# A hybrid DeltaNet and retention layer on one Trainium2 core: TensorE's order from the v convolutions to the last merge written out by hand

## The chip, the core and the metric

The kernel runs on one NeuronCore of a Trainium2 chip. Its engines run side by side, each through its own list of instructions in order: TensorE (PE, matrix products; PEld is its weight load), VectorE (DVE), ScalarE (ACT), GpSimd (POOL) and SyncE (SP, which here only issues DMAs). They wait for each other through semaphores. The metric is the device time in microseconds; lower is better.

## What is computed

One layer over 256 context and 1024 latent tokens of width 1024, float32 in and out: a modulated RMSNorm, one input projection, two parallel head groups (gated DeltaNet and retention, each in both directions), an output projection, and a SwiGLU block. The part that matters here is the first head group up to its triangular solves, and the columns of the projection that belong to gates:

```
qkv_a, z, ab, rq, rk, rv, rg = jnp.split(p, splits, axis=-1)
qkv_a = concat([short_conv(qkv_a[:, :CTX_LEN], cw), short_conv(qkv_a[:, CTX_LEN:], cw)])   # 5 taps, then silu
q = l2_normalize(q) * (HEAD_DIM ** -0.5);  k = l2_normalize(k)
...
G = jnp.cumsum(gc, axis=-1)
decay = jnp.where(incl, jnp.exp(G_i - G_j), 0.0)
A = jnp.where(strict, einsum('nbhid,nbhjd->nbhij', kb, kc) * decay, 0.0)
sol = triangular_solve(A + I, rhs)          # per chunk of 64 tokens, head and direction
qk = einsum('nbhid,nbhjd->nbhij', qc, kc) * decay
...
o_gdn = rms_norm(o_f + o_b) * silu(z);   o_ret = head_group_norm(r_f + r_b) * silu(rg)
```

## The kernel before

The 1280 tokens are ten tiles of 128 (0 and 1 the context, 2 to 9 latent). Activations stand as `hhi`/`hlo` and weights as `whi`/`wlo`, two parts of a split float32, so each product is three matmuls. The input projection is made in two forms. **Convolved columns** come from `conv_block` (L605 to L618): twelve blocks of 128 columns (q, k, v of four heads; the v heads are blocks 8 to 11), each in chunks of 256, 512 and 512 tokens; ACT copies the chunk from PSUM into `u` (L608) and, with the middle tap, into `y` (L609), DVE adds the four other taps (L615), ACT applies Silu (L618). **Token-major columns** come from `token_major` (L371 to L373, tile `tm`): ten groups `g` of 256 columns; 2 to 5 are retention's q and k with rotary (`fin_rope`), 6 and 7 the retention gate `rg`, 8 and 9 the gate `z`, both finished with a Silu on ACT (`fin_gate`, L532) into `res`, of which there are two buffers, and stored to DRAM.

`ada_rest` sums a modulation vector: DVE accumulates eight slices of a weight read from DRAM into `acc` (L497, L499), one matmul `gr` (L504) adds across partitions. The last of these, `gr_2313`, and the q transposes `qt` (L686, with squares on ACT, L688) stand just ahead of the section that is changed.

**Preparation** (`pre`, per tile): load `kc` and `qc` (normalised k and q, from DRAM, L659), `kk` = k·kᵀ (L724) and `kq` (L729) for four heads, and for either direction the decay `e`: load `gw` (L732), a triangular mask on POOL (L736), four Exp on ACT (L740). DVE multiplies, `ut` = kk·e (L744) and `sp` = kq·e (L746). `ut` goes to DRAM (`un`, L747), `sp` too (`sd`, L749).

**Inversion** (`invert`, per batch of tiles): `un` is read back in another layout, 32 x 32 blocks, into `yr` (L763), copied into `L` (half on DVE, L771, half on ACT, L770), and 31 double steps on DVE (L777, L779) invert all diagonal blocks of the batch at once; the number of steps doesn't depend on how many tiles the batch has. `X` and its transpose `XT` (L781) go to DRAM (`xd`, L783).

**Merge** (`merge`, per batch): blocks are read back (`U` from `un` and `xd`, `t` from `xd`, L795 to L800), small matmuls `m` on PE make 64 x 64 blocks (L819, then L826 and L829) and 128 x 128 blocks (L842, L846), with a negation on DVE between (L822, L843) and copies on ACT (L832, L835, L848). The result is stored; the scans, from L913 on (`pk`, then `Tr` on PE, L944), need it.

PSUM has three banks for `tm` and `vT`, three for `gr`, `qt`, `kk`, `kq` and `m`, two for the convolution. `vT` (L868) are the transposes of a v head, ten per head, copied by ACT (`vt`, L870) and stored.

The program is written as a list, and a scheduler orders each engine by a timeline that it simulates, in which the list is only the starting point; matmuls of groups 8, 9 and later ones thus fill waits of the preparation. In the list stand: groups 6 and 7; `solve` of batches 0 and 1 (four tiles each); four v heads with their transposes; `pre` of batch 2 (tiles 5, 6); merge 0, inversion 2, merges 1 and 2; groups 8 and 9.

Of the kernel before, what the change touches and what calls it, by code (L numbers as in the profile page):

```python
# [2 lines left out]

# [14 lines left out]
P = 128  # L18
# [7 lines left out]
H = 4  # L26
# [12 lines left out]
def build(nc, tc, ap, dbg=None, stop=None, marks=None):  # L39
# [53 lines left out]
    def bank_b(name):  # L93
        return bank("pb", name)
# [96 lines left out]
    try:  # L191
# [197 lines left out]
        def token_major(g, tiles, finish, store, pl, q=S):  # L389

            w = [tm_weights(g, kh, pl, q) for kh in range(2)]

            for p in range(0, len(tiles), 2):
                pair = [(t, tm_bank(g)) for t in tiles[p:p + 2]]
                for kh in range(2):
                    for t, o in pair:
                        tm_half(o, w[kh], kh, t)
                for t, o in pair:
                    tm_store(g, t, o, finish, store, pl)

        def fin_copy(t, o, res):
            S.activation(res, o, AF.Copy)
# [190 lines left out]
        close(AB)  # L593
        CV = pool("cv", side="right")

        def conv_block(b, y, lat):
# [3 lines left out]
            for c0, n in (CHUNKS[1:] if lat else CHUNKS):  # L600
# [8 lines left out]
                S.activation(y[:, c0:c0 + n], o, AF.Copy, scale=cw[:, b, 2:3])  # L609
            segs = [(NCTX, NLAT)] if lat else [(0, NCTX), (NCTX, NLAT)]  # L610
            for i, e in ((0, V), (1, V), (3, V), (4, V)):
                for s0, n in segs:
                    sh = i - 2
                    lo, hi = s0 + max(0, -sh), s0 + n - max(0, sh)
                    e.scalar_tensor_tensor(y[:, lo:hi], u[:, lo + sh:hi + sh], cw[:, b, i:i + 1], y[:, lo:hi],  # L615
                                           ALU.mult, ALU.add)
            a0 = NCTX if lat else 0
            S.activation(y[:, a0:], y[:, a0:], AF.Silu)  # L618

        def newy():  # L620
            return CV.tile([P, NTOK], F32, tag="y", name="y", bufs=3)
# [97 lines left out]
        def pre(t):  # L719
            b, c = where[t]  # L720
            kc = load(GP, kd[t], "kc", 2)
            pk = bank_b("kk")
            for h in range(H):
                T.matmul(pk[:, h * P:(h + 1) * P], kc[:, h, :], kc[:, h, :], start=True, stop=True)  # L724
            if t >= 2:
                qc = load(GP, qd[t - 2], "qc", 2)
                pq = bank_b("kq")
                for h in range(H):
                    T.matmul(pq[:, h * P:(h + 1) * P], kc[:, h, :], qc[:, h, :], start=True, stop=True)  # L729
            for d in range(2):  # L730
                gw = GP.tile([P, H, P], F32, tag="gw", name="gw", bufs=2)
                SY.dma_start(gw.rearrange("p h i -> p (h i)"),  # L732
                             grow_d[c8(t, d), :].rearrange("a b -> (a b)").partition_broadcast(P))
                e = GP.tile([P, H, P], F32, tag="e", name="e", bufs=2)
                sg = 1 if d == 0 else -1
                G.affine_select(out=e, in_=gw, compare_op=ALU.is_ge, fill=FAR, base=0,  # L736
                                pattern=[[0, H], [sg, P]], channel_multiplier=-sg)
                for h in range(H):
                    col = t * 8 + d * 4 + h
                    S.activation(e[:, h, :], e[:, h, :], AF.Exp, bias=sm["nG"][:, col:col + 1])  # L740
                if t >= 2:
                    sp = GP.tile([P, H, P], F32, tag="sp", name="sp", bufs=2)
                ut = GU.tile([P, H, P], F32, tag="ut", name="ut", bufs=2)
                V.tensor_tensor(ut.rearrange("p h i -> p (h i)"), pk, e.rearrange("p h i -> p (h i)"), ALU.mult)  # L744
                if t >= 2:
                    V.tensor_tensor(sp.rearrange("p h i -> p (h i)"), pq, e.rearrange("p h i -> p (h i)"), ALU.mult)  # L746
                SY.dma_start(un[b][:, 1 - d, c * H:(c + 1) * H, :], ut)  # L747
                if t >= 2:
# [55 lines left out]
        def merge(b):  # L804

            uu, ub, t64 = blocks(b)
            nu = len(BATCH[b]) * H
# [12 lines left out]
                             start=True, stop=True)  # L820
            xt1 = GM.tile([P, 16, 32], F32, tag="xt1", name="xt1", bufs=1)
            V.tensor_scalar(xt1.rearrange("p n j -> p (n j)")[:, :nu * 32], ps1[:, :nu * 32], -1.0, None, ALU.mult)  # L822
            ps2, ps3 = bank_b("m1"), bank_b("m1")
            for n in range(nu):
                for d, p, a, bb in pairs:
# [5 lines left out]
            for d, p, a, bb in pairs:  # L831
                S.activation(u[d][q[a], :, q[bb]], three(ps2[:, :nu * 32], q[a], 32), AF.Copy)  # L832
                if p == d:
                    ca = (a % 2) * 32
                    S.activation(t[d][q[bb], :, ca:ca + 32], three(ps3[:, :nu * 32], q[bb], 32), AF.Copy)  # L835
            halves = [(0, slice(0, 64), slice(64, 128)), (1, slice(64, 128), slice(0, 64))]
            for n0 in range(0, nu, 8):
                ps1, ps2 = bank_b("m2"), bank_b("m2")
                xt2 = GM.tile([P, 8, 64], F32, tag="xt2", name="xt2", bufs=1)
                for n in range(8):  # L840
                    for d, A, B in halves:
                        T.matmul(ps1[B, n * 64:n * 64 + 64], u[d][A, n0 + n, B], t[d][A, n0 + n, :], start=True, stop=True)  # L842
                V.tensor_scalar(xt2.rearrange("p n j -> p (n j)"), ps1, -1.0, None, ALU.mult)  # L843
                for n in range(8):
                    for d, A, B in halves:
                        T.matmul(ps2[A, n * 64:n * 64 + 64], xt2[B, n, :], u[d][B, n0 + n, B], start=True, stop=True)  # L846
                for d, A, B in halves:
                    S.activation(u[d][A, n0:n0 + 8, B], three(ps2, A, 64), AF.Copy)  # L848
            for c, t in enumerate(BATCH[b]):
# [3 lines left out]
        def solve(b):  # L853
            for t in BATCH[b]:
                pre(t)
            checkpoint("pre%d" % b)
            invert(b)
            checkpoint("inv%d" % b)

        solve(0)  # L860
        solve(1)
        for h in range(H):
            y = newy()
            conv_block(8 + h, y, False)
            for t0, n in ((0, 2), (2, 4), (6, 4)):
                ps = bank_a("vT")
                for t in range(t0, t0 + n):
                    T.transpose(ps[:, (t - t0) * P:(t - t0 + 1) * P], y[:, t * P:(t + 1) * P], ident)  # L868
# [3 lines left out]
        close(CV)  # L872
        checkpoint("v")
        RP = pool("rp", side="right")
        rope = RP.tile([P, TT, P], F32, tag="rope", name="rope")
        GM = pool("gm", side="right")
        for t in BATCH[2]:
            pre(t)
        close(GP)
        G2 = pool("g2")  # L880
        checkpoint("pre2")
        merge(0)
        SY.dma_start(rope, ap["rope"])
        invert(2)
        checkpoint("inv2")
        merge(1)
        merge(2)


        for g in (8, 9):  # L890
            token_major(g, LAT, fin_gate, S, W)
        checkpoint("rgz")
        close(GM)
        close(G2)
# [778 lines left out]
```

## Time and profile before

| | |
|---|---|
| time, median of 3 runs | 1481.7 us (1480.53 to 1482.51) |
| the profiled execution | 1482.3 us |
| its span, first to last instruction | 1480.4 us |
| mean granted TensorE clock | 0.981 |
| last matmul of group 6 ends | 248.6 us |
| last matmul of the merges ends | 474.7 us |
| DVE busy | 981.1 us (66%) |

Times within the execution are counted from the span's start. A row of the timeline has start, duration, engine, line, operation, output<-input with shapes, and in brackets the idle time of the engine ahead of it and what ended that. A row of the grouped view has busy time and mean ns of one, then the idle time ahead of the group by releaser. The rest of the profile's slices, by tenths of the span:

```profile
PE   7999999997889999998799899999999999999997
DVE  6568797379772535789677886746555554657586
ACT  5543554765222111446444533323333333454454
```

The section that is changed lies in the seventh to thirteenth slice of 37 us, where PE's digits fall to 7 and 8.

### The profile page before, as it was taken

The numbers are of one execution on the slowest core, as the hardware profiler recorded it, in microseconds if no ns is written. First come the engines' busy times: TensorE is split into PE (matmuls) and PEld (weight loads), VectorE is DVE, ScalarE is ACT, GpSimd is POOL, SyncE is SP. The second block draws the span as 40 slices with busy tenths as digits, with TensorE's granted clock in tenths as the row PEclk, the third lists the DMA queues.
The fourth block names the chain that finished last, engine by engine and source line by source line (L and its number), as shares of the span: only waits on it lengthen the run. The fifth ranks groups of instructions, "written<-read, shape, count | busy, mean of one in ns | idle before, by whom it ended". The sixth has DMA issues, their size and how long they took to land.

```text
span 1480.4 us, 24179 instructions
## 1 busy us (share of the span) xinstructions
PE 1399.8 (95%) x8919; PEld 1200.6 (81%) x8919; DVE 981.1 (66%) x1909; ACT 610.5 (41%) x1336; POOL 579.5 (39%) x493
## 2 busy tenths in 40 slices
PE   7999999997889999998799899999999999999997
PEld 2798888876879999898588688877888888788886
DVE  6568797379772535789677886746555554657586
ACT  5543554765222111446444533323333333454454
POOL 0130010220102353254135588999555553335321
PEclk9999999999899999999799999999999999999999
DMA  9537686696878625985633265765232242786863
GB/s 338 186 104 230 178 245 204 199 297 191 256 193 272 247 69 185 411 328 181 217 115 115 85 215 210 266 240 178 107 107 107 107 150 74 239 279 195 306 202 114
DMA packets 170710, 293.95 MB, mean 199 GB/s; under 512 B 43528, under 2 KB 93912, under 8 KB 166496
## 3 DMA queue, kind: packets, MB, share of 16 engines
q1 hardware_dynamic: 119040, 248.98, 49.3%
q10 hardware_dynamic: 49072, 35.83, 7.7%
q0 software_dynamic: 2480, 7.60, 1.4%
q8 instruction: 70, 1.15, 0.3%
q14 instruction: 48, 0.39, 0.1%
HBM read 206.60 MB, written 85.77 MB: 197 GB/s over the span
## 4 chain that ended last, share of the span: by engine, by line
PE 40%; POOL 6%; DMA 2%; issue 1%; DVE 1%; ACT 0%; POOLq 0%; DVEq 0%; ACTq 0%
PE ffn L1362 7%; PE ffn L1360 6%; PE ffn L1361 6%; PE fo L1486 5%; PE fo L1488 5%; PE fo L1487 5%; DMA wd<-tw 2%; PE op L1219 2%; PE op L1220 2%; PE op L1221 2%; POOL ws L1333 1%; POOL tw L1414 1%; POOL tw L1413 1%; POOL tw L1416 1%; POOL tw L1415 1%
## 5 line engine op out<-in xcount | busy, mean ns | idle before, releaser
L371 PE MATMUL tm<-whi,hhi 128*128 128x256 f32 (+1 forms) x704 | 200.8, 290 | 7.2 <-ACT res L532 3.6
L372 PE MATMUL tm<-wlo,hhi 128*128 128x256 f32 (+1 forms) x704 | 200.4, 287 | 1.3 <-DVE wlo L345 1.3
L373 PE MATMUL tm<-whi,hlo 128*128 128x256 f32 (+1 forms) x704 | 198.7, 287 | 0.0
L371 PEld LDWEIGHTS tm<-whi,hhi 128*128 128x128 f32 x704 | 133.9, 192 | 11.5 <-ACT res L532 4.0
L1360 PE MATMUL ffn<-t,whi 128*128 128x512 f32 x352 | 136.9, 390 | 1.3 <-ACT whi L344 1.3
L1362 PE MATMUL ffn<-t,wlo 128*128 128x512 f32 x352 | 137.0, 390 | 0.8 <-DVE wlo L345 0.8
L372 PEld LDWEIGHTS tm<-wlo,hhi 128*128 128x128 f32 x704 | 134.9, 192 | 3.1 <-DVE wlo L345 1.7
L1361 PE MATMUL ffn<-t,whi 128*128 128x512 f32 x352 | 137.0, 389 | 0.0
L344 ACT ACTIVATE whi<-wraw 128x512 fp32r<-128x512 f32 (+2 forms) x98 | 75.1, 770 | 147.9 <-PE ffn L1361 81.9
L373 PEld LDWEIGHTS tm<-whi,hlo 128*128 128x128 f32 x704 | 134.2, 192 | 0.6 <-DVE hlo L314 0.2
L344 ACT ACTIVATE whi<-ws 128x512 fp32r<-128x512 f32 x88 | 55.6, 632 | 172.5 <-PE ffn L1361 131.3
L345 DVE TENSOR_TENSOR wlo<-ws,whi 128x512 fp32r<-128x512 f32 x88 | 94.0, 1069 | 46.5 <-ACT whi L344 46.3
L1486 PE MATMUL fo<-whi,ahi 128*128 128x512 f32 x308 | 119.3, 389 | 0.7 <-ACT ahi L344 0.7
L1487 PE MATMUL fo<-wlo,ahi 128*128 128x512 f32 x308 | 119.9, 389 | 0.0
L1488 PE MATMUL fo<-whi,alo 128*128 128x512 f32 x308 | 119.0, 390 | 0.0
L345 DVE TENSOR_TENSOR wlo<-wraw,whi 128x512 fp32r<-128x512 f32 (+2 forms) x92 | 100.7, 1097 | 23.4 <-ACT whi L344 23.4
L1360 PE MATMUL ffn<-b,whi 128*128 128x512 f32 x264 | 104.1, 394 | 4.1 <-ACT whi L344 4.1
L1362 PE MATMUL ffn<-b,wlo 128*128 128x512 f32 x264 | 103.9, 393 | 0.7 <-DVE wlo L345 0.7
L1361 PE MATMUL ffn<-b,whi 128*128 128x512 f32 x264 | 103.7, 393 | 0.0
L605 PE MATMUL b<-hhi,whi 128*128 128x512 f32 (+1 forms) x256 | 94.7, 370 | 0.8 <-ACT y L609 0.8
L607 PE MATMUL b<-hhi,wlo 128*128 128x512 f32 (+1 forms) x256 | 94.6, 370 | 0.0
L606 PE MATMUL b<-hlo,whi 128*128 128x512 f32 (+1 forms) x256 | 93.8, 366 | 0.0
(451 smaller groups left out, 3422.0 us busy)
## 6 DMA issues: line engine op xcount, KB each, us to landing
adaw<-ada SPq DMA_DIRECT2D x48, 512.0 KB, 4.6
pk<-sd SPq DMA_DIRECT2D x16, 1536.0 KB, 15.1
wraw<-wfi SPq DMA_DIRECT2D x44, 512.0 KB, 4.5
ar<-ad SPq DMA_DIRECT2D x33, 512.0 KB, 4.4
w<-wfo SPq DMA_DIRECT2D x22, 512.0 KB, 3.6
wd<-tw SPq DMA_DIRECT2D x11, 1024.0 KB, 4.9
ad<-act SPq DMA_DIRECT2D x20, 512.0 KB, 3.2
raw<-wd SPq DMA_DIRECT2D x20, 512.0 KB, 4.8
```

The costliest lines, as they stand in the source:

```text
L344: S.activation(hi, raw, AF.Copy)
L345: e.tensor_tensor(lo, raw, hi.bitcast(F32), ALU.subtract)
L371: T.matmul(o, hhi[:, k, tsl], whi[:, k % 4, :], start=(k == 0), stop=False)
L372: T.matmul(o, hhi[:, k, tsl], wlo[:, k % 4, :], start=False, stop=False)
L373: T.matmul(o, hlo[:, k, tsl], whi[:, k % 4, :], start=False, stop=(k == KT - 1))
L605: T.matmul(o, whi[:, k, :], hh, start=(k == 0), stop=False)
L1360: T.matmul(o, whi[:, k, :], xhi(xn, slice(0, 4), k), start=(first and k == 0), stop=False, **kw)
L1361: T.matmul(o, whi[:, k, :], xlo(xn, slice(0, 4), k), start=False, stop=False, **kw)
L1362: T.matmul(o, wlo[:, k, :], xhi(xn, slice(0, 4), k), start=False, stop=(k == 3), **kw)
L1486: T.matmul(po[g][i], ahi[:, ts], whi, start=(j == 0 and not kw), stop=False, **kw)
L1487: T.matmul(po[g][i], ahi[:, ts], wlo, start=False, stop=False, **kw)
L1488: T.matmul(po[g][i], alo[:, ts], whi, start=False, stop=(j == FH - 1), **kw)
```

## The change

The section is written anew. TensorE alone runs in the written order there (`tc.manual_schedule`); the other engines are ordered by the scheduler as before. `conv_block`, `token_major` and `merge` become generators, which are run piece by piece: `conv(h)` runs two chunks of a v head or the last one, `filler(n)` runs n half pairs of tiles (24 matmuls each) of groups 7, 8 and 9. Group 7 no longer stands ahead of the section, but is filler too, with its weights loaded through ACT's queue rather than SP's. `pre` is cut into `pre_load`, which is written one chunk ahead, and `pre_mm`; `gw` and `e` get three buffers instead of two. The batches are tiles [0, 1], [2, 9, 3, 8] and [4, 7, 5, 6] where they were [0, 1, 2, 9], [3, 8, 4, 7] and [5, 6].

```
-        token_major(7, LAT, fin_gate, S, W2, SY)
...
-        BATCH = [[0,1,2,9],[3,8,4,7],[5,6]]
+        BATCH = [[0, 1], [2, 9, 3, 8], [4, 7, 5, 6]]
...
-                gw = GP.tile([P, H, P], F32, tag="gw", name="gw", bufs=2)
+                gw = GP.tile([P, H, P], F32, tag="gw", name="gw", bufs=3)
...
+        with tc.manual_schedule(engines={mybir.EngineType.PE}):
...
+            fill = chain.from_iterable(tm_steps(g, LAT, fin_gate, S, W) for g in (7, 8, 9))
...
+            pre_load(0)
+            conv(0)
+            conv(0)
+            pre_load(1)
+            pre_mm(0)
+            conv(1)
+            pre_load(2)
+            pre_mm(1)
+            invert(0)
+            conv(1)
+            vturn(0, ys[0])
+            pre_load(9)
+            pre_mm(2)
...
+            pre_mm(8)
+            invert(1)
+            conv(3)
+            vturn(2, ys[2])
+            pre_load(7)
+            pre_mm(4)
+            filler(2)
+            pre_load(5)
+            pre_mm(7)
+            filler(2)
+            vturn(3, ys[3])
...
+            pre_load(6)
+            pre_mm(5)
+            filler(2)
+            pre_mm(6)
...
+            invert(2)
+            SY.dma_start(rope, ap["rope"])
+            filler(2)
+            for b in range(3):
+                for _ in merge_steps(b):
+                    filler(1)
+                if b == 1:
+                    filler(3)
+            filler(99)
```

What this moves on the engines, at three places. A row has the line, the operation, and output<-input with the numbers of the buffers. First TensorE, where group 6 (`tm_2691`) ends. Before, group 7 (`tm_2832`, `tm_2833`) stands there and `gr_2313` in its last quarter:

```order
L373 MATMUL tm_2833<-whi_2764,hlo_87 128x256
L373 MATMUL tm_2832<-whi_2770,hlo_87 128x256
L371 MATMUL tm_2833<-whi_2770,hhi_86 128x256
L372 MATMUL tm_2833<-wlo_2771,hhi_86 128x256
L373 MATMUL tm_2833<-whi_2770,hlo_87 128x256
L371 MATMUL tm_2833<-whi_2770,hhi_86 128x256
L504 MATMUL gr_2313<-acc_2296,ones_81 1x512
L686 MATMUL qt_2320<-ident_65,y_2138 128x128 x4
```

After the change, with the lines' new numbers (`gr` is L511, `qt` L699, the convolution L614 to L616):

```order
L372 MATMUL tm_2691<-wlo_2517,hhi_86 128x256
L373 MATMUL tm_2691<-whi_2516,hlo_87 128x256
L511 MATMUL gr_2313<-acc_2296,ones_81 1x512
L699 MATMUL qt_2320<-ident_65,y_2138 128x128 x4
L699 MATMUL qt_2329<-ident_65,y_2138 128x128 x4
L699 MATMUL qt_2406<-ident_65,y_2229 128x128 x4
L699 MATMUL qt_2415<-ident_65,y_2229 128x128 x4
L614 MATMUL b2_2810<-hhi_86,whi_2803 128x256
```

`gr_2313` moved from the last quarter of group 7 to the place right behind group 6, and v's first chunk follows.

Second ACT, near the last v head's transposes. Before, the Exp of two directions (`e_4128`, `e_4144`) stand together:

```order
L870 ACTIVATE vt_3935<-vT_3930 128x512
L740 ACT_TABLE_LOAD
L740 ACTIVATE e_4128<-e_4128,nG_1284 128x128 x4
L740 ACTIVATE e_4144<-e_4144,nG_1284 128x128 x4
L871 DMA sd_1296<-vt_3935 128x4x128
L618 ACT_TABLE_LOAD
L618 ACTIVATE y_3938<-y_3938 128x1280
```

After the change group 7's Silu stores (`res`, L539) stand between them (Exp is L748, the v head's Silu L627):

```order
L627 ACTIVATE y_3457<-y_3457 128x1280
L748 ACT_TABLE_LOAD
L748 ACTIVATE e_3864<-e_3864,nG_1284 128x128 x4
L539 ACT_TABLE_LOAD
L539 ACTIVATE res_3944<-tm_3894 128x256
L748 ACT_TABLE_LOAD
L748 ACTIVATE e_3986<-e_3986,nG_1284 128x128 x3
L539 ACT_TABLE_LOAD
L539 ACTIVATE res_3947<-tm_3895 128x256
L748 ACT_TABLE_LOAD
L748 ACTIVATE e_3986<-e_3986,nG_1284 128x128
L885 ACTIVATE vt_3953<-vT_3950 128x256
```

Each change between Exp and Silu now has a table load: 18 in this part of ACT's rows, 8 before.

Third DVE, at the copy of the first inversion's input (`L_3178` before, `L_3036` after). Before, it stands among convolution taps and products of other tiles:

```order
L345 TENSOR_TENSOR wlo_3820<-wraw_3821,whi_3819 128x8x128
L615 SCALAR_TENSOR_TENSOR y_3578<-u_3585,cw_1293,y_3578 128x1022
L744 TENSOR_TENSOR ut_3354<-kk_3331,e_3345 128x512
L615 SCALAR_TENSOR_TENSOR y_3578<-u_3585,cw_1293,y_3578 128x1023
L771 COPY L_3178<-yr_3173 64x1024
L615 SCALAR_TENSOR_TENSOR y_3698<-u_3705,cw_1293,y_3698 128x254
L615 SCALAR_TENSOR_TENSOR y_3578<-u_3585,cw_1293,y_3578 128x1023
```

After the change (taps L624, `ut` L765, `sp` L769, copy L792, inversion L798):

```order
L624 SCALAR_TENSOR_TENSOR y_2933<-u_2940,cw_1293,y_2933 128x254
L765 TENSOR_TENSOR ut_3024<-kk_3019,e_2904 128x512
L765 TENSOR_TENSOR ut_3027<-kk_3019,e_2914 128x512
L792 COPY L_3036<-yr_3031 32x1024
L624 SCALAR_TENSOR_TENSOR y_2933<-u_2940,cw_1293,y_2933 128x1022
L765 TENSOR_TENSOR ut_3233<-kk_3223,e_3001 128x512
L765 TENSOR_TENSOR ut_3239<-kk_3223,e_3011 128x512
L769 TENSOR_TENSOR sp_3236<-kq_3228,e_3001 128x512
L769 TENSOR_TENSOR sp_3242<-kq_3228,e_3011 128x512
L798 TENSOR_TENSOR tmp_3042<-L_3036,X_3037 64x31
```

The copy now comes directly behind the products that it is made from (`ut_3024`, `ut_3027`, which go out to DRAM as `un` and come back as `yr_3031`), with all of v's large taps but the first head's behind it.

More of the change, by code (lines that the diff above doesn't have):

```diff
@@ L1 @@
 from contextlib import ExitStack, nullcontext
-from itertools import zip_longest
+from itertools import chain, zip_longest
 import numpy as np
@@ L397, in token_major @@
                         tm_half(o, w[kh], kh, t)
+                    if kh == 0:
+                        yield
                 for t, o in pair:
                     tm_store(g, t, o, finish, store, pl)
+                yield
+        def token_major(g, tiles, finish, store, pl, q=S):
+            for _ in tm_steps(g, tiles, finish, store, pl, q):
+                pass
         def fin_copy(t, o, res):
@@ L618, in conv_block @@
             S.activation(y[:, a0:], y[:, a0:], AF.Silu)
+        def conv_block(b, y, lat):
+            for _ in conv_steps(b, y, lat):
+                pass
         def newy():
@@ L712, in build, with pre_load @@
         GP = pool("gp")
-        BATCH = [[0,1,2,9],[3,8,4,7],[5,6]]
+        BATCH = [[0, 1], [2, 9, 3, 8], [4, 7, 5, 6]]
         where = {t: (b, c) for b, ch in enumerate(BATCH) for c, t in enumerate(ch)}
         un = [dr.tile([P, 2, len(ch) * H, P], F32, tag="un%d" % b, name="un%d" % b) for b, ch in enumerate(BATCH)]
-        def pre(t):
-            b, c = where[t]
+        ready = {}
+        def pre_load(t):
             kc = load(GP, kd[t], "kc", 2)
[L722 to L729, printed above, removed]
+            es = []
             for d in range(2):
-                gw = GP.tile([P, H, P], F32, tag="gw", name="gw", bufs=2)
+                gw = GP.tile([P, H, P], F32, tag="gw", name="gw", bufs=3)
                 SY.dma_start(gw.rearrange("p h i -> p (h i)"),
                              grow_d[c8(t, d), :].rearrange("a b -> (a b)").partition_broadcast(P))
-                e = GP.tile([P, H, P], F32, tag="e", name="e", bufs=2)
+                if d == 0:
+                    qc = load(GP, qd[t - 2], "qc", 2) if t >= 2 else None
+                e = GP.tile([P, H, P], F32, tag="e", name="e", bufs=3)
                 sg = 1 if d == 0 else -1
@@ L740, in pre, with pre_mm @@
                     S.activation(e[:, h, :], e[:, h, :], AF.Exp, bias=sm["nG"][:, col:col + 1])
+                es.append(e)
+            ready[t] = kc, qc, es
+        def pre_mm(t):
+            b, c = where[t]
+            kc, qc, es = ready.pop(t)
+            pk = bank_b("kk")
+            for h in range(H):
+                T.matmul(pk[:, h * P:(h + 1) * P], kc[:, h, :], kc[:, h, :], start=True, stop=True)
+            if t >= 2:
+                pq = bank_b("kq")
+                for h in range(H):
+                    T.matmul(pq[:, h * P:(h + 1) * P], kc[:, h, :], qc[:, h, :], start=True, stop=True)
+            for d in range(2):
+                e = es[d].rearrange("p h i -> p (h i)")
+                ut = GU.tile([P, H, P], F32, tag="ut", name="ut", bufs=2)
+                V.tensor_tensor(ut.rearrange("p h i -> p (h i)"), pk, e, ALU.mult)
+                SY.dma_start(un[b][:, 1 - d, c * H:(c + 1) * H, :], ut)
                 if t >= 2:
                     sp = GP.tile([P, H, P], F32, tag="sp", name="sp", bufs=2)
[L743 to L748, printed above, removed]
+                    V.tensor_tensor(sp.rearrange("p h i -> p (h i)"), pq, e, ALU.mult)
                     SY.dma_start(sd[t, :, 8 - 8 * d], sp.rearrange("p h i -> p (h i)"))
@@ L802, in blocks, with merge_steps @@
             return uu, [uu[:, 1 - d] for d in range(2)], [tt[:, d] for d in range(2)]
-        def merge(b):
+        def merge_steps(b):
             uu, ub, t64 = blocks(b)
@@ L843, in merge @@
                 V.tensor_scalar(xt2.rearrange("p n j -> p (n j)"), ps1, -1.0, None, ALU.mult)
+                yield
                 for n in range(8):
@@ L851, in merge, with vturn @@
             checkpoint("mrg%d" % b)
[L853 to L864, printed above, removed]
+        def vturn(h, y):
             for t0, n in ((0, 2), (2, 4), (6, 4)):
@@ L871, in build @@
                 S.dma_start(vd[t0:t0 + n, :, h, :].rearrange("t p j -> p t j"), vt[:, :n])
[L872 to L891, printed above, removed]
+        with tc.manual_schedule(engines={mybir.EngineType.PE}):
+            ys, vg = [], []
+            def conv(h):
+                if h == len(vg):
+                    ys.append(newy())
+                    vg.append(conv_steps(8 + h, ys[h], False))
+                next(vg[h], None)
+            fill = chain.from_iterable(tm_steps(g, LAT, fin_gate, S, W) for g in (7, 8, 9))
+            def filler(n):
+                for _ in range(n):
+                    next(fill, None)
+            pre_load(0)
[11 more added lines that the diff above has]
+            pre_mm(2)
+            conv(2)
+            pre_load(3)
+            pre_mm(9)
+            conv(2)
+            vturn(1, ys[1])
+            pre_load(8)
+            pre_mm(3)
+            conv(3)
+            pre_load(4)
+            pre_mm(8)
+            invert(1)
+            conv(3)
+            vturn(2, ys[2])
[6 more added lines that the diff above has]
+            vturn(3, ys[3])
+            close(CV)
+            RP = pool("rp", side="right")
+            rope = RP.tile([P, TT, P], F32, tag="rope", name="rope")
+            GM = pool("gm", side="right")
+            pre_load(6)
+            pre_mm(5)
+            filler(2)
+            pre_mm(6)
+            close(GP)
+            G2 = pool("g2")
+            invert(2)
[7 more added lines that the diff above has]
+            filler(99)
```

12 lines of the change are left out of this document (9 added, 3 removed).

## The prediction

> **What bounds the kernel now.** I read the page's totals first: TensorE (PE) is busy for 95% of the span, so only its idle time can be won or lost. Then I asked for busy time by stretch, cut where the changed section begins and ends; the columns are the stretch, its length, then busy time and count of PE, PEld, DVE, ACT and POOL, the granted TensorE clock, the DMA share and GB/s.
> ```profile
> PE 1399.8 (95%) x8919; PEld 1200.6 (81%) x8919; DVE 981.1 (66%) x1909; ACT 610.5 (41%) x1336; POOL 579.5 (39%) x493
> ...
> 248.60:474.70 226.10, 196.59 (x2336) 180.69 (x2336) 150.29 (x302) 103.52 (x258) 32.79 (x42) 0.95 0.75 226
> ...
> 360.00:370.00 10.00, 1.10 (x10) 0.91 (x9) 9.45 (x14) 6.08 (x12) 2.20 (x2) 0.82 0.70 223
> 370.00:380.00 10.00, 7.36 (x47) 7.36 (x48) 9.11 (x27) 3.19 (x4) 1.81 (x1) 0.67 0.96 341
> ...
> 560.00:575.00 15.00, 15.00 (x130) 15.00 (x129) 5.09 (x18) 0.00 (x0) 8.29 (x18) 1.00 0.21 79
> ```
> The first stretch runs from the last matmul of column group 6 to the last matmul of the last merge: this is what the change rewrites, and PE is idle there for 226.10 − 196.59 = 29.5 us. Afterwards, around 560 to 575, PE is never idle, so what is gained or lost before 475, and what matmul work is left over for afterwards, reaches the end of the kernel one for one.
>
> Next the list of PE's waits (total, times, longest) and the timeline at the largest one.
> ```profile
> PE vT L868 <- ACT y L618: 13.1, 3, 11.5
> PE m L829 <- issue: 4.5, 2, 3.4
> PE tm L371 <- ACT res L532: 3.6, 2, 2.7
> ...
> 371.32 1.27 ACT L618 ACTIVATE y<-y 128x1280 f32<-128x1280 f32 x1 [3.69 <-DVE y L615]
> 372.64 2.40 PE L868 MATMUL vT<-ident,y 128*128 128x128 f32 x10 [11.54 <-ACT y L618]
> 374.01 1.14 DVE L781 COPY XT<-X 128x1024 f32<-128x1024 f32 x1
> ```
> One wait makes up 11.5 of the 29.5: the transposes of the last v head stand until DVE has done the last tap of its convolution, since the scheduler ran DVE's inversion steps beside it. A written TensorE order can put gate columns (L371) there. That is the gain on offer.
>
> **What goes: up to 29.5 us, and 11.5 of it surely moves.** The amount of matmul work is the same, but 124 tm matmuls fewer stand ahead of the last merge's end (1383 before, 1259 now), so they come later.
> ```profile
> 251.00:259.00 8.00, 8.00 (x70) 8.00 (x69) 4.55 (x7) 0.77 (x2) 0.00 (x0) 1.00 0.52 167
> 351.00:356.00 5.00, 5.00 (x24) 4.03 (x22) 4.93 (x11) 2.93 (x4) 0.00 (x0) 1.00 0.24 72
> ```
> The first row is tm alone: seventy touch 8 us, two or three only at an edge, 0.119 each, so 124 are 14.8 us. (The second is convolution alone, 0.23 each of 512 columns; a v head's 48 of these and 24 of 256 are 14 us.) The merges of before end at 474.7; to break even they must now end at **474.7 − 14.8 = 460**. What follows is therefore a sum for that moment.
>
> **First new wait: gr.** The matmul `gr_2313` (L504, now L511), which ends a sum over eight weight slices, used to stand in the middle of group 7's matmuls; now it comes right behind group 6, with the q transposes and all of v behind it on PE.
> ```profile
> 253.79 1.54 DVE L499 SCALAR_TENSOR_TENSOR acc<-adaw,csl,acc 128x512 f32<-128x512 f32 x2 [1.21 <-DMA adaw<-ada]
> 255.97 1.54 DVE L499 SCALAR_TENSOR_TENSOR acc<-adaw,csl,acc 128x512 f32<-128x512 f32 x2 [0.65 <-DMA adaw<-ada]
> ```
> DVE ended that sum at 257.5; without group 7's two weight splits of 1.2 beside it I take 255.8 (bounds 254 to 257.5). Group 6 ends at 248.6, so PE idles **7.2 us**; the cover, group 7, is gone from here.
>
> **Second: the first inversion's input.** From 255.8 PE runs gr, the q transposes and v0 (to about 275), tile 0's kk, two chunks of v1, tile 1's kk at about 285; DVE multiplies its second `ut` by about 288.5. In DVE's new order the copy of L comes directly behind, ahead of the rest of the convolutions. The path of before gives its delay:
> ```profile
> 297.60 0.69 DVE L744 TENSOR_TENSOR ut<-kk,e 128x512 f32<-128x512 f32 x1 [1.36 <-DMA un<-ut]
> 298.32 0.32 SPq L747 DMA_DIRECT2D un<-ut  x1
> 302.82 4.90 SPq L763 DMA_DIRECT2D yr<-un  x4
> 310.38 1.12 DVE L771 COPY L<-yr 64x1024 f32<-64x1024 f32 x1
> ```
> From the end of ut (298.3) through DRAM and back it is 12.1 us until L, and other DVE work filled that time. Now L stands in front of it: DVE idles until about **300.6**. Behind L, DVE has, up to XT, which ends the first inversion:
> ```profile
> L615 DVE SCALAR_TENSOR_TENSOR y<-u,cw,y 128x1022 f32<-128x1022 f32 (+3 forms) x40 | 39.9, 1004 | 2.4 <-ACT y L609 2.1
> L779 DVE TENSOR_TENSOR X<-X,tmp 128x31 f32<-128x31 f32 (+23 forms) x93 | 34.7, 373 | 2.7
> L777 DVE TENSOR_TENSOR tmp<-L,X 128x31 f32<-128x31 f32 (+23 forms) x93 | 31.7, 341 | 2.7
> L744 DVE TENSOR_TENSOR ut<-kk,e 128x512 f32<-128x512 f32 x20 | 13.5, 685 | 25.6 <-POOL X L767 9.7 <-DMA un<-ut 8.5 <-ACT e L740 7.4
> L345 DVE TENSOR_TENSOR wlo<-wraw,whi 128x1024 fp32r<-128x1024 f32 x9 | 11.0, 1219 | 13.5 <-ACT whi L344 13.5
> L781 DVE COPY XT<-X 128x1024 f32<-128x1024 f32 (+1 forms) x3 | 3.2, 1076 | 0.1
> ```
> One inversion of three, (31.7 + 34.7)/3 = 22.1; half of the convolution taps, 20.0; 32 products like ut at 0.685, 21.9; two weight splits, 2.4; two copies, 2.2: 68.6 busy. Neighbours overlap by some 0.08, which takes 4 off 54 large ones: 64.3. So XT would end at 300.6 + 64.3 = 365 if DVE never waited again.
>
> **Third: table loads.** Group 7's Silu stores (L539) now alternate on ACT with the Exp of the decays (L748). ACT's rows hold 18 table loads in the section for 8 before.
> ```profile
> 319.37 1.28 ACT L740 ACT_TABLE_LOAD   x1
> 320.66 2.45 ACT L740 ACTIVATE e<-e,nG 128x128 f32<-128x128 f32 x8
> L740 ACT ACT_TABLE_LOAD x4 | 5.1, 1283 | 0.1
> ```
> Ten more at 1.28 are 12.8 us, all between the last v chunk and v3's transposes. That chunk ends at about 333: 255.8, 5 for gr and the q transposes, 56 for four heads, 11 for five tiles' products and two heads' transposes, 5 for waits. With 24 Exp of 0.31, five stores, one Silu and three vt, ACT has some 25 us there: v3's transposes end about 360 where PE could have had them 6 us sooner, and the kk of the last two tiles stands behind them on PE. DVE runs dry for about 6 to 7 us. **XT of the first inversion ends at about 372** (it was 375, although v starts almost 20 us sooner).
>
> Here the Trainium skill, "ScalarE: Activation LUTs", What ACT_TABLE_LOAD costs, speaks against the change more strongly: a switch of set takes the load of 1283 ns and a drain of about 1380 ns. By it ten switches are 26.6 us; the rows just above show Exp 1.29 us after its load began and no drain behind it, so the sum goes by 1.28.
>
> **Fourth: the merges.** A merge's matmuls need X and XT written to DRAM and read back.
> ```profile
> 410.16 1.05 DVE L781 COPY XT<-X 128x1024 f32<-128x1024 f32 x1
> ...
> 416.19 2.43 SPq L799 DMA_DIRECT2D U<-xd  x3
> ...
> 421.43 0.63 SPq L800 DMA_DIRECT2D t<-xd  x1
> ...
> 434.38 1.29 PE L819 MATMUL m<-t,U 32*32 32x32 f32 x128
> ...
> 473.58 1.15 PE L846 MATMUL m<-U,xt 64*64 64x64 f32 x32
> ```
> XT ended at 411.2, the last read was issued at 421.4 and lands some 3 us later, so 13.4 us (12 to 15). Before, gate and rope columns hid it (the matmuls began only at 434). Now PE has run group 7 by about 374, and the first merge is next in the written order: it stands until 372 + 13.4 = 385, a wait of **12 us**. DVE's second inversion needs a copy, 22.1, two splits and the merge's two negations, 29 us: XT at 401, second merge at 414.5. Between the two, PE has 72 tm (8.6) and a small merge (4), ready at 398: a wait of **16**. Both waits, and that of gr, cannot be filled, since TensorE's order is fixed. Behind them nothing waits any more: 324 tm (38.7), two merges of 16 units (m1 1.3, the next step 2.2, four groups of 1.14: 8.1 each) and about 3 of switching, 58 us.
>
> **Sum.** Merges end at XT + 29 + 13.4 + 58 = XT + 100.4 = 472.4, against 460: **+12 us**. As a check by idle time: 7 + 6 + 12 + 16 = 41 for 29.5. The profiled execution took 1482.3 (span 1480.4), 0.6 above the median of the runs; 1482.3 + 12 = **1494**. Taking group 7's tail, `e` and `gw` with three buffers for two, and the rope load moved behind the third inversion, at nothing: the first two only let loads start sooner, and rope is used at 480 and later; each could add what a wait on SP's queue takes, 1 to 5 us, and those ends are in the range.
>
> The other rule I weigh is "TensorE: Matmul & The Clock Gate", What's actually happening, of the Trainium skill: an idle window of some 3.4 us halves the clock until a busy one. The 0.67 granted at 370 to 380 agrees. Three gaps over that length now for two or three before would change the sum by 1 or 2 us only.
>
> **Rivals.**
> *Faster.* The point is where XT of the first inversion ends: 460 − 100.4 = **360**. If DVE never idles at L (other work is done before it, or un and yr take little, as two tiles move half of what four did), XT ends at 288.5 + 64.3 = 353; the first merge is then ready when PE is, the second still waits 15, and the merges end at 453: −7, **1475**. For it: PE's largest wait of before is gone, and this inversion needs two tiles, not four. Against it: DVE's written position of L, and its 64 us of work behind it. No stall at all would give 1482.3 − 29.5 = 1453.
> *No change.* XT at 360 within 3: the new waits take what the old one gave, **1482**.
> *Worse.* ACT is late by another 10 us (each table switch dearer than the rows show, or the res buffers, two of them, hold up PSUM): XT at 382, **1504**.
> *The change does nothing.* The orders of PE and ACT differ as told, so no chance is kept for it.
>
> **How the numbers follow.** Slower by about 12: 0.60, itself 1486 to 1501 by the bounds on gr (3), the round trip (3) and XT (5). Worse: 0.12. No change: 0.10. Faster: 0.18. Slower by over 0.2% (3 us, about what a measurement of this kernel can tell) is 0.72, the same 0.10, faster 0.18. The range 1474 to 1507 reaches both outer rivals and leaves out half of the faster one and a little above.
>
> **What would show it.** In the profile after: PE idle about 7 us before gr; DVE idle about 12 before L; 18 table loads with vT waiting on ACT; m1 of the first two merges waiting 12 and 16; the merges' end at 472. XT of the first inversion before 360 would make me wrong, and so would m1 that never waits.

## The result, and the profile after

| | before | after |
|---|---|---|
| time, median (4 runs each) | 1481.97 us (1480.53 to 1482.51) | 1521.37 us (1517.2 to 1522.14) |
| ratio after/before | | **1.0262** (95%: 1.0241 to 1.0282) |
| the profiled execution, its span | 1482.3, 1480.4 us | 1517.2, 1515.4 us |
| mean granted TensorE clock | 0.981 | 0.967 |
| first inversion's XT ends | 375.2 | 375.1 |
| last matmul of the merges ends | 474.7 | 490.1 |
| output projection starts on PE | 719.3 | 758.3 |

The change makes the kernel 2.6% slower, 39 us at the median; it was forecast slower by 12. (The profiled execution after is the quickest of its four, so its rows explain 35 of them.)

First PE's busy time in three stretches: from group 6 to the last merge, on to the output projection, and to the end. The kernel after:

```profile
246.00:490.06 244.06, 191.25 (x2231) 173.76 (x2230) 147.68 (x291) 118.23 (x269) 32.57 (x30) 0.87 0.73 219
490.06:758.30 268.24, 243.88 (x2022) 240.15 (x2021) 172.92 (x575) 86.27 (x249) 112.20 (x157) 0.96 0.60 221
758.30:1515.40 757.10, 737.39 (x3276) 606.59 (x3276) 484.66 (x682) 293.35 (x524) 414.25 (x282) 0.99 0.50 171
```

The same three for the kernel before:

```profile
246.00:474.76 228.76, 199.24 (x2351) 182.19 (x2349) 152.04 (x305) 104.96 (x260) 32.79 (x42) 0.96 0.75 227
474.76:719.30 244.54, 225.72 (x1906) 221.14 (x1906) 163.05 (x549) 81.77 (x241) 101.40 (x143) 0.99 0.67 245
719.30:1480.40 761.10, 741.12 (x3276) 608.63 (x3276) 486.07 (x693) 296.46 (x532) 415.96 (x284) 0.99 0.49 170
```

The second column is the length, the third PE's busy time, the third from the end its granted clock. PE's idle time in the first stretch went from 29.5 to 52.8: **+23.3**. Its busy time there fell by 8.0 only, though 14.8 us of gate columns left the stretch: the same work took **6.8** longer, and the clock column says why (0.87 for 0.96: PE was busy for 31 us at half clock in this stretch, before for 13, so the clock can have cost up to 9). In the second stretch idle time grew by **5.5** (24.4 for 18.8), and busy time by 18.2, of which 14.8 are those columns and **3.4** go with the lower clock (0.96 for 0.99). The third is **4.0** shorter. 23.3 + 6.8 + 5.5 + 3.4 − 4.0 = 35.0, the difference of the spans. (The last stretch, with its 3276 matmuls, lasts 754 to 764 us in all the traces of this case but one, x_vg's; differences of this size there are not explained by the section.)

What PE waited for in the first stretch, by the list of its waits after (total, times, longest):

```profile
PE m L840 <- DMA t<-xd: 29.1, 8, 13.6
PE gr L511 <- DVE acc L506: 8.4, 1, 8.4
PE vT L883 <- ACT res L539: 6.7, 2, 3.8
PE tm L371 <- ACT vt L885: 2.9, 1, 2.9
PE tm L373 <- issue: 2.5, 1, 2.5
```

The wait for v's Silu, 11.5 before, is gone, as the change intends. Four others have come, and over half of them is one: the first matmuls of a merge (L840) wait for their operands from DRAM. The timeline at these places:

```profile
288.12 1.28 DVE L765 TENSOR_TENSOR ut<-kk,e 128x512 f32<-128x512 f32 x2
297.73 1.11 DVE L792 COPY L<-yr 32x1024 f32<-32x1024 f32 x1 [8.33 <-DMA yr<-un]
...
373.98 1.10 DVE L802 COPY XT<-X 64x1024 f32<-64x1024 f32 x1
...
377.84 0.31 SPq L804 DMA_DIRECT2D xd<-XT  x1
...
379.24 7.10 SPq L784 DMA_DIRECT2D yr<-un  x4
386.44 2.12 SPq L820 DMA_DIRECT2D U<-xd  x1
...
391.21 0.28 PE L840 MATMUL m<-t,U 32*32 32x32 f32 x2 [13.57 <-DMA t<-xd]
394.08 1.06 PE L840 MATMUL m<-t,U 32*32 32x32 f32 x58 [0.88 <-DMA t<-xd]
...
406.29 1.28 DVE L802 COPY XT<-X 128x1024 f32<-128x1024 f32 x1
...
418.52 0.28 PE L840 MATMUL m<-t,U 32*32 32x32 f32 x2 [9.61 <-DMA t<-xd]
423.34 1.91 PE L840 MATMUL m<-t,U 32*32 32x32 f32 x122 [1.98 <-DMA t<-xd]
```

From XT to the first merge's last operand it is 19 us, not 13.4: the first write of XT goes out 2.8 us after XT has ended, and the reads U and t stand behind four reads yr for the third inversion in SP's queue, which took 7.1 to issue. At the second merge, with no such reads ahead, it is 16. PE stands 15.5 us in four pieces, then 13.5 us at the second merge. The ten microseconds around the end of each wait have half the clock:

```profile
388.00:398.00 10.00, 4.82 (x77) 4.39 (x78) 6.62 (x17) 0.00 (x0) 0.00 (x0) 0.50 0.87 230
418.00:428.00 10.00, 5.56 (x141) 5.13 (x142) 7.80 (x19) 0.00 (x0) 0.00 (x0) 0.50 0.99 261
```

In the second stretch two waits are new, both in the retention's last tiles, far from any edited line:

```profile
PE ro L1164 <- DMA vg<-rd: 7.5, 1, 7.5
...
PE ru L1106 <- DMA vg<-rd: 4.3, 1, 4.3
```

The scheduler still orders that part, and it ordered it differently than before (a load of `vg` goes out at 747.77, just when POOL ends its reading of the oldest buffer, 746.48 + 1.26).

### The profile page after: what moved, and what is told of

It reads as the page before. It is cut to its first block, busy times and chain, and to the rows that moved or that the text cites. A ratio compares the mean times of both kernels' runs of the same rounds, so it can differ in the third digit from the quotient of the medians.

```text
span 1515.4 us, 24191 instructions
## 1 busy us (share of the span) xinstructions
PE 1407.1 (93%) x8919; PEld 1209.5 (80%) x8919; DVE 985.6 (65%) x1909; ACT 625.4 (41%) x1346; POOL 588.4 (39%) x493
## 5 line engine op out<-in xcount | busy, mean ns | idle before, releaser
L345 DVE TENSOR_TENSOR wlo<-wraw,whi 128x512 fp32r<-128x512 f32 (+2 forms) x92 | 105.0, 1142 | 36.5 <-ACT whi L344 36.4
L614 PE MATMUL b<-hhi,whi 128*128 128x512 f32 (+1 forms) x256 | 94.6, 370 | 0.0
L616 PE MATMUL b<-hhi,wlo 128*128 128x512 f32 (+1 forms) x256 | 94.4, 369 | 0.0
```

What stands on the lines that cost most here:

```text
L345: e.tensor_tensor(lo, raw, hi.bitcast(F32), ALU.subtract)
```

## The experiments

The theory after the first look: the written order is the loss, because nothing can pass a merge's matmuls while their operands travel through DRAM, and the slow clock adds to it. Rivals: the new batches; the new list and its loads; group 7's new place (`gr` without cover, table loads); the retention's new order. Ratios below are to the kernel before, timed beside each, with 95% intervals.

**The written order taken away (x_auto).** The list, the batches and group 7 stay as changed:

```
-        with tc.manual_schedule(engines={mybir.EngineType.PE}):
+        with nullcontext():
```

> The changed program without TensorE's written order (the scheduler orders TensorE too; list, batches and group 7 as changed). If the fixed order is what costs (the merges' first matmuls cannot be passed by gate columns), the waits of m1 for the DRAM round trip (29 us in the changed kernel) are filled and the time falls to 1475-1490. If the new batches or the new list cost, TensorE's order aside, it stays above 1505.

1497.33 us, ratio 1.0107 (1.0085 to 1.0128). That lies between the two cases: 24 of the 39 us are the written order's, about 15 are not. PE's waits in the section:

```profile
PE m L840 <- DMA t<-xd: 10.3, 6, 3.7
PE m L848 <- issue: 8.5, 3, 4.9
PE gr L511 <- DVE acc L506: 8.0, 1, 8.0
PE tm L371 <- ACT res L539: 3.4, 1, 3.4
```

The merges' waits are 10 instead of 29; `gr` still waits 8.0. The waits for `vg` are gone too: the retention is ordered nearly as before.

**The batches alone (x_batch)**, in the kernel before:

```
-        BATCH = [[0,1,2,9],[3,8,4,7],[5,6]]
+        BATCH = [[0, 1], [2, 9, 3, 8], [4, 7, 5, 6]]
```

> The kernel before with nothing but the new batches (tiles 0, 1; then 2, 9, 3, 8; then 4, 7, 5, 6). If the batches are harmless in themselves: 1475-1490. If the larger last batch (four tiles where it had two) delays the end of the merges: 1495 or more, by the later third merge.

1486.48, ratio 1.0031 (1.0015 to 1.0048): 5 us, nearly harmless. Its merges end at 489.6, as late as those of the changed kernel, and yet it starts the projection at 721.8: the scheduler had put more gate and rotary columns ahead. When the merges end says little unless the work done by then is counted with it.

**Group 7's place alone (b_g7late)**, in the kernel before (its weights then come through ACT's queue):

```
-        token_major(7, LAT, fin_gate, S, W2, SY)
...
-        for g in (8, 9):
+        for g in (7, 8, 9):
```

> The kernel before with nothing changed but group 7, which goes from its place ahead of the section to the gate groups 8 and 9 at the end of the list. If gr without cover costs (8 us of PE idle) and v starts that much sooner in exchange, the two nearly cancel: within 4 of 1482. If the move is part of what the changed kernel loses (gr's wait and Silu among the Exp, 20 table loads or so), 1488 or more.

1495.18, ratio 1.0071 (1.0059 to 1.0084): 11 us from this alone. PE's waits:

```profile
PE vT L867 <- ACT y L618: 11.4, 2, 10.3
PE gr L504 <- DVE acc L499: 8.9, 1, 8.9
PE m L825 <- issue: 5.5, 2, 3.2
PE tm L371 <- ACT vt L869: 5.3, 1, 5.3
```

`gr` without its cover waits 8.9, near the 7.2 that were predicted, and v's earlier start doesn't pay for it: the old wait for v's Silu is still 10.3 long. Table loads are not what costs here: the section has 10 of them, for 8 before.

**Group 7 back in the changed kernel (x_g7)**: the line above restored, filler from groups 8 and 9 only, none among the preparation and none between the third inversion and the first merge.

> The changed kernel with group 7 back ahead of the section (in front of gr, its weights through SP), so no Silu among the Exp and no wait of PE at gr. If waits simply add up, 8.4 (gr) and 9.9 (v transposes and gate columns behind ACT) go: about 1503. If the chain ut, inversion, XT, merge sets the time, v and with it XT only start 15 us later, the first merge's matmuls wait some 30 us for their operands instead of 15, and it stays at 1518 to 1528.

1534.13, ratio 1.0335 (1.0312 to 1.0359): 13 slower than the changed kernel and above both expected cases. Waits do not add up; the chain through the inversion sets the time, as the second case had it:

```profile
PE m L841 <- DMA t<-xd: 25.9, 6, 21.2
PE m L841 <- DVE tmp L799: 18.7, 1, 18.7
PE vT L884 <- ACT y L627: 11.6, 1, 11.6
```

The wait at `gr` is gone, XT comes 13 us later (387.9), and the merges' first matmuls wait 45 us (the list splits them by what ended last). With this fixed order, work moved ahead of v delays the whole chain and leaves less to put behind it; how much of the 13 is the filler that is missing ahead of the first merge was not tried apart.

**Group 7 behind the last tile (x_late)**: the three `filler(2)` among the last four tiles taken out, and eight half pairs in place of two behind the third inversion.

> The changed kernel with all eight half pairs of group 7 behind the last tile's kk and kq, none between the last four tiles. If group 7's Silu among the Exp (ten more table loads, banks held) delays the first inversion, its XT ends some 7 us sooner (367), all three merges come as much sooner and the time is about 1513; the wait of m1 for the first merge shrinks too. If ACT's table loads are not on the path, it stays within 3 of the changed kernel's 1521.

1517.16, ratio 1.0242 (1.0218 to 1.0265), not clear of the changed kernel's 1.0262. Half of the expectation held: XT of the first inversion came 7.4 us sooner and the first merge's matmuls at 383 instead of 394. But the second merge came no sooner:

```profile
366.62 1.11 DVE L802 COPY XT<-X 64x1024 f32<-64x1024 f32 x1
...
422.38 0.28 PE L840 MATMUL m<-t,U 32*32 32x32 f32 x2 [20.30 <-DMA t<-xd]
```

DVE waited 10.6 us for the weights of the gate groups (`wlo` behind `whi`), which stand in its order among the second inversion's steps, so its XT ended only 2 us sooner (405.6). From there to the second merge's last operand it then took 21 us for 16 (two of the reads `t` alone 6.1 to issue, for 2.0). So group 7's columns among the last tiles cost the first inversion about what the prediction said, and the next waits took the gain. That it is their table loads is likely, but not shown: the section has 12 loads for 18, but the run also moved 144 matmuls, some 17 us of PE, out of the last tiles' way.

**Filler moved into the second gap (x_gap)**:

```
-                if b == 1:
+                if b == 0:
                     filler(3)
```

> The changed kernel with the three half pairs (72 matmuls, 8.8 us) that follow the second merge put between the first and the second merge, nothing else. If TensorE's wait ahead of the second merge is the loss, 8.8 of its 13.5 us are filled and the merges end 7 to 9 us sooner: about 1513. If the merges are bound by the chain of inversions, XT to XT on DVE, and the third merge then waits instead, the gain is under 3: 1518-1522.

1513.1, ratio 1.0213 (1.0188 to 1.0238), 8 us less for moving 72 matmuls. The second merge's four waits shrank from 13.5 to 5.7. In the program nothing but the place of these matmuls differs, so this much of the loss at the merges is idle time for want of something in the written order.

**The written order filled (x_full)**: group 7 ahead of the section, no filler among the preparation, 8 half pairs ahead of the first merge, 7 and 2 behind the first and second, and rotary groups 2 and 3 as further filler:

```
+            fill = chain(chain.from_iterable(tm_steps(g, LAT, fin_gate, S, W) for g in (8, 9)),
+                         chain.from_iterable(tm_steps(g, ALL, fin_rope, G, W) for g in (2, 3)))
...
+            filler(8)
...
+                if b < 2:
+                    filler((7, 2)[b])
```

> TensorE's order still written, but filled by the traces: group 7 ahead of the section, none among the preparation, then 8 half pairs ahead of the first merge, 7 between first and second, 2 between second and third, one per step as before, with rotary groups 2 and 3 as further filler behind the gate groups. If the loss is that nothing stood in the written order to fill the waits for the DRAM round trip, m1 waits under 10 us in all, and the time is 1465 to 1490 (the wait for vg may stay, about 10). If the inversions' chain itself is what came too late, filler cannot help and it stays above 1505.

1501.63, ratio 1.0126 (1.0094 to 1.0157), between the two cases, 12 above the better one. The merges' waits fell to 7.5, as expected, but others stayed:

```profile
PE vT L884 <- ACT y L627: 11.6, 1, 11.6
PE m L841 <- DMA t<-xd: 7.5, 5, 2.4
PE tm L371 <- ACT res L539: 7.2, 2, 6.4
```

So half of the loss was to be had, 32 us against x_g7, which has group 7 in the same place but less filler. The wait for v's Silu is back, since nothing stands ahead of it.

**The list without the written order and with group 7 in its old place (x_autog7).**

> The changed program without TensorE's written order and with group 7 back ahead of the section; what is left of the change is the new batches, the new order of the list (loads of a chunk ahead, three buffers for gw and e, inversions ahead of the merges). If the parts add up (batches alone 4, group 7 alone 11, written order 24 of 39), the time is that of the kernel before plus 4: 1484 to 1490. If the new list has a cost of its own, it is 1492 or more.

1497.09, ratio 1.0106 (1.0083 to 1.0128). The parts do not add up: batches and new list together cost 14 us, the batches alone 5, and in the new list group 7's place makes no difference (x_auto has 1.0107). That the new list costs some 10 us by itself is a difference (14 less 5), right only if the two add; which of its pieces (loads one chunk ahead, three buffers, where the inversions stand) was not tried apart. In its trace PE waits 6.6 us for a `kc` load at one tile, where the kernel before waits 1.2.

**The retention's wait for vg (x_vg, b_vg)**: `"vg", 4` made `"vg", 5` at its three loads, in the changed kernel and in the one before.

> The changed kernel with five buffers for the retention tiles vg where it has four, nothing else. After the merges PE waits 7.5 and 4.3 us for vg there (not in the kernel before), since each load waits until POOL has used the oldest buffer. If that is a cost of its own, 8 to 11 us go: the output projection starts at about 748 instead of 758, time about 1511. If another wait stands right behind (qk, the states), the gain is under 3: 1518 or more.

> The kernel before with five vg buffers. It has no wait for vg on PE, so it stays within 3 of 1482 if the wait belongs to the order of the changed program; if four buffers bind in both, it falls to about 1475.

x_vg: 1519.11, ratio 1.0237 (1.02 to 1.0275), no clear gain; b_vg: 1480.18, ratio 0.9989 (0.9968 to 1.001). In x_vg's trace both waits are gone and the second stretch is 8.0 shorter, though the scheduler reordered the retention once more and `ro` waits 6.4 for DVE in it:

```profile
493.46:753.70 260.24, 240.19 (x2018) 236.38 (x2018) 164.48 (x570) 82.25 (x240) 107.90 (x155) 0.97 0.61 224
753.70:1520.70 767.00, 742.26 (x3280) 609.76 (x3280) 479.26 (x686) 295.57 (x532) 416.36 (x283) 0.98 0.50 170
...
PE yT L1268 <- DMA yt<-dy: 5.4, 2, 5.2
```

The stretch behind it is 9.9 longer. Half of that is a wait of 5.2 at 767.8, 14 us into the stretch, where the projection needs the retention's output `yt` (0.3 in the changed kernel); the other half is PE's busy time and was not settled. So the 8 us are won where the wait stood, but the retention's last store goes out at 764.3 as in the changed kernel (764.4), and the end of the kernel did not get them.

**Keeping the clock up (x_warm)**: 110 matmuls that nobody reads ahead of the first merge, 75 ahead of the second.

> The changed kernel with idle work: 110 matmuls whose result nobody reads ahead of the first merge and 75 ahead of the second, where PE waits for the round trip anyway. No useful work is filled in, so if only idle time counts the time stays at 1521 or grows by a few. If the clock that PE gets after those waits (0.50 for 10 us each in the changed kernel) is a cost of its own, the matmuls behind them run at full pace and 3 to 6 us go: 1515 to 1518.

1531.64, ratio 1.032 (1.0305 to 1.0335), outside both cases. The idle matmuls ended at 392.5, the operands then came in over 4 us, and the gate columns behind took 4.62 us for 24, as without them (4.66). The second merge's reads also came 7 to 12 us later, so that the 75 matmuls there had ended 10 us before the operands came. The clock was 0.88 in the ten microseconds from 398, although PE had been busy up to 392.5. The run says nothing on the price of the clock; that stays an account of busy time.

**One place of the old kernel's order written (b_fill)**: the kernel before, with two pairs of tiles of group 8 ahead of the last v head's transposes, the place of its largest wait.

```
+            with (tc.manual_schedule(engines={mybir.EngineType.PE}) if h == H - 1 else nullcontext()):
+                if h == H - 1:
+                    zg8 = tm_steps(8, LAT, fin_gate, S, W)
+                    for _ in range(4):
+                        next(zg8)
                 for t0, n in ((0, 2), (2, 4), (6, 4)):
```

> The kernel before with one place of TensorE's order written: two pairs of tiles of gate group 8 (96 matmuls, 11.5 us) stand ahead of the last v head's transposes, where PE stood 11.5 us for ACT's Silu. If an idle stretch of PE is worth its length wherever ready work is put into it, and the slow clock behind it goes too, the time falls by 8 to 12, to about 1472. If the first merge only comes later by as much (its buffers take the place of v's), it stays within 3 of 1482.

**1467.95 us, ratio 0.9898 (0.9883 to 0.9914): faster than both kernels**, by more than the 11.5 us of the wait. The windows that read 1.10 and 7.36 before:

```profile
360.00:370.00 10.00, 10.00 (x87) 9.91 (x86) 8.89 (x13) 7.00 (x15) 2.20 (x2) 1.00 0.75 231
370.00:380.00 10.00, 9.24 (x77) 8.73 (x76) 9.21 (x25) 3.74 (x6) 1.81 (x1) 1.00 0.94 323
```

PE is full, at full clock, where it stood and then ran at 0.67. The first inversion came hardly later (XT at 376.1, 375.2 before). But the gain did not go straight to the end. The merges end at 470.7, 4.1 sooner, and PE has done 100 gate and rotary matmuls (11.9 us) more by then, so 16.0 us are won there: 11.0 of idle time and 5.0 of busy time. Of these 6.5 are lost again in the next stretch, where PE now waits 8.0 for `vg` at one tile, as the changed kernel does, since the scheduler reordered the retention here too. The last stretch, 754.1 for 761.1, gives 7.0 back. That 1% is won is measured; that it equals what was won at the filled wait is in part luck.

## Why the prediction was right in sign and wrong in size

The forecast was slower by 12, at 1494, with an upper bound of 1507; measured were 39, at 1521, outside the range. Step by step:

- **What bounds, and the wait that goes:** right. The 11.5 us are gone, and b_fill shows that filling this place alone pays. But "one for one" held only roughly: the changed kernel was 30.1 us behind at the merges' end (15.3 later, 14.8 of work less) and 35.0 at the end, and b_fill's 16.0 went down to 9.5 before the last stretch made them 16.5.
- **`gr`:** 7.2 predicted, 8.4 measured (8.9 in b_g7late); DVE was done at 255.5, as predicted, but group 6 had ended at 247.1, not 248.6.
- **L:** DVE to stand until 300.6; it waited 8.3 and had L at 297.7.
- **Table loads:** 18 as counted, 1.28 each (`PE vT` and `tm` behind ACT: 9.6 for the 6 predicted). XT of the first inversion 372 predicted, 375.1 measured. The Trainium skill, "ScalarE: Activation LUTs", What ACT_TABLE_LOAD costs, would have a drain of 1.38 us more at each; after too the Exp starts 1.30 us after its load began (351.61 and 352.91), so the row decides again:

```profile
351.61 1.28 ACT L748 ACT_TABLE_LOAD   x1
352.91 1.28 ACT L748 ACTIVATE e<-e,nG 128x128 f32<-128x128 f32 x4
```

- **The merges' waits:** 12 and 16 predicted, 15.5 and 13.5 measured, 28 against 29 together. That the sum agrees is luck, as the moments were off: at the second merge PE stood ready at 408.9 (398 predicted) and the last operand came at 423.3 (414.5). The round trip took 19 and 16 for 13.4; in the first, SP's queue held the third inversion's four reads ahead of the merge's. The rows of before had them ahead as well (yr at 376.98, U and t only from 392); I took the second merge's round trip, which had nothing ahead of it.
- **The stretch behind the second merge:** 58 predicted, 66.7 measured (423.3 to 490.1). I let nothing wait there and counted every matmul at full clock; the trace has 4.5 us of idle time, and a clock of 0.50 in two pieces (423.3 to 429.3 and 470.3 to 477.1) in which PE was busy for 12.5 us.

**The step that failed** is the sum for the merges' end, XT + 29 + 13.4 + 58 = 472.4: they ended at 490.1, 17.7 later. XT gives 3.1 of this; the way from there to the second merge's last operand 5.8 (48.2 for 42.4: the second inversion 32.5 for 29, its round trip 15.8 for 13.4); the stretch behind, which was mis-sized most, 8.7. The check by idle time shows the same from its side: of 41 for 29.5 it came to 52.8, 12 more, of which 6.0 are the items above at their measured size (8.4 + 9.6 + 15.5 + 13.5 = 47.0 for 41) and 5.8 small waits that I left out (2.5 and 1.7 on issue the largest). Two things had no term in the sum at all. **The clock:** the windows above show 0.50 for the ten microseconds around the end of each merge's wait, and the same work took 6.8 us longer in the section and 3.4 in the next stretch, where I allowed 1 or 2. I had weighed the rule of "TensorE: Matmul & The Clock Gate", What's actually happening, in the Trainium skill, that an idle window halves the clock until a busy one; the windows agree with it, but my price for it was too low. A likely reason, argued and not tested apart: the operands come in pieces, so that PE works only now and then for some microseconds behind each wait (x_warm's clock fell behind such pieces too). **The rest of the kernel:** I took it as unchanged behind the section, and the scheduler reordered the retention: 5.5 us more idle there, and the last stretch came out 4.0 shorter.

The rivals: *worse* (1504) had the right direction with the wrong cause, a later XT; XT was on time. *Faster* could not come about as its point, XT at 360, was missed by 15; and x_late, with XT at 367.7, shows that this point decided less than I thought, since the second merge's operands didn't follow.

What stays open: which part of the new list costs some 10 us without the written order (x_autog7), how much of the retention's new order reaches the end (x_vg, b_fill), and why the last stretch is some microseconds shorter or longer.

## What to carry to other kernels

A fixed order for one engine took away its answer to the DRAM round trip here: before writing one, count for each wait in it the microseconds of ready work that stand in front, and write the order only where a trace shows a wait and ready work beside it. Here one such place (b_fill) gave 1%, and the whole section written out cost 24 us, 1.6% (x_auto). Price a wait of PE with the slow clock behind it, and compare kernels by work done at a moment, not by when a stage ends.

## What the runs showed that I had not expected

- A part of the program that no edit touches can change its order when a scheduler simulates the whole: the retention's last tiles wait 11.8 us for `vg` in the changed kernel and not in x_auto, which differs in one line of the section before. So an edit's gain is measured only together with such a reordering (b_fill waits 8.0 there).
- The granted clock around the end of a wait of 9.6 to 13.6 us was 0.50 for ten microseconds; in b_fill, where one 11.5 us wait is filled with work, the mean clock is 0.990 for 0.981 and the kernel 15 us faster.
